# Early mLSTM convolutions, rotary tables on 128x128, and a planner that treats VectorE and GpSimd as exclusive

## The chip, the cores and the metric

The kernel runs on one core of a Trainium2 chip. The metric is the device time of one execution in microseconds (us); lower is better. A core has a matrix engine (TensorE, PE in the profile, with its weight loads as PEld), three engines for elementwise work (VectorE is DVE, ScalarE is ACT, GpSimd is POOL), and SyncE (SP), whose queue issues all the DMAs here. Each engine works through its own instructions in order and waits on semaphores of the others. Matmul results land in PSUM banks; all other tiles lie in SBUF.

## The reference

512 tokens of width 1024 pass through two blocks, all in float32. In the first, `u = rms_norm(h)` is multiplied by `w_in`, and the product is cut into the inputs of two mixers:

```python
# latent attention (MLA), 4 heads of 128 + 64 rotary columns
cos, sin = rope_cos_sin(positions)     # ang = positions[..., None] * inv_freq, 32 frequencies
q_pe, k_pe = apply_rope(q_pe, cos, sin), apply_rope(k_rope, cos, sin)
mla_out = causal_mla(q, k, v)
# mLSTM, 4 heads of 128
qk = silu(causal_dwconv(concat([m_q, m_k]), conv_w, conv_b))   # 4 taps, 1024 channels
hm = mlstm_chunkwise(mq, mk, m_v, m_i + gate_bias_i, m_f + gate_bias_f)
mlstm_out = sigmoid(m_o) * rms_norm(hm, mlstm_norm)
mix = concat([mla_out, mlstm_out]) @ w_out
```

A SwiGLU feed-forward part, a gated embedding and a second block of two layers (differential attention, a short convolution, and two squared-ReLU feed-forward parts) follow. They are most of the time and no line of theirs is changed.

## The kernel before

**Products.** A float32 matrix is split into a high and a low part (`hi` by a ScalarE copy, `lo = x - hi` by VectorE or GpSimd), and each product is three matmuls: `hi*hi`, `hi*lo` and `lo*hi` (`mm3`, L344 to L346). Weights arrive as `raw` tiles (six of them, 128x512, loaded over SP's queue), are split into `whl` tiles by the `converter`, and are multiplied by the split activations `a`. So each weight costs ScalarE a copy and VectorE or GpSimd a subtraction (L303) before PE can use its low part.

**The order of the work.** The program is written as many Python generators ("streams"). While it is built, a planner (`Sched`) keeps a clock for each engine, has a cost formula for each operation, and at each step emits the operation that can start first by its estimate; ties go by a stream's priority. That fixes each engine's order of instructions, and SP's queue of DMAs too. On the chip an engine can't leave that order: where an estimate was too short, everything behind it waits. A request `"vg"` (from `tt`, used for the low parts) can go to VectorE or to GpSimd; `start` compares their estimated ends with a handicap, `tune(("vg", s.shared), 0.2)`, which is -0.2 while `s.shared` is false and 0.2 once it is true. Requests of `stt`, `vtt` and `tt` carry a flag that both inputs lie in SBUF (`two`). Only from `block1_rest` on, when `s.shared` is set, is a GpSimd operation planned as excluding such a VectorE operation, by the clock `s.port`.

**The first 240 us**, which the change touches: `x_in` reads and splits x; `z_in`, `v_block` and `z_main` multiply by `w_in`. `rope_tables` (priority 2) builds the cosine table `C` and the sine table `Sn` from positions and frequencies: `positions` is broadcast to all 128 partitions, and a chain of dependent GpSimd operations on 128x512 (`pts`, a scaling; `ptt`, an addition) brings the angles into the range of the sine: 13 `pts` and 8 `ptt`. Then VectorE clamps and ScalarE makes `Sn` and `C`. The frequencies repeat every 32 partitions, so the 128 rows of `C` are four equal groups. `rope_key` and `rope_q` wait for the key `"rope"`; the rotated queries go through a DMA (`qr<-p`) before `scores` of the attention can use them. `main1` runs `z_main` for four conv inputs (tiles 0, 4, 1, 5, kept as `rawz` in `a` tiles) during the attention, and after `"roped"` for the other four (in `y` tiles) and four output gates; these projections are PE's reserve while the mixers wait for other engines.

When the attention is done its pool is closed, the mLSTM pool is opened, and `conv_silu` runs for the tiles 0, 4, 1, 5, 2, 6, 3, 7: one ScalarE instruction, three multiply-adds on VectorE (L316), a tanh on ScalarE, a last VectorE instruction, and the split into `qk`. `mlstm_core` of head h needs `qk` of the tiles h and 4 + h. Its decay matrix `bc` comes by DMA; `decay` adds the triangular mask `tri` on GpSimd (`ptt`, L312) and takes the exponent on ScalarE; `weigh` multiplies the scores in PSUM by it.

## Time and profile before

| | us |
|---|---|
| three runs: median (lowest to highest) | 1825.43 (1823.6 to 1826.53) |
| the profiled execution | 1826.98 |
| its span from first to last instruction | 1825.2 |
| PE busy in it | 1785.4 |
| VectorE busy | 1372.8 |
| ScalarE busy | 1007.5 |
| GpSimd busy | 208.8 |

The profiled execution took 1.8 us more than its span, and 1.55 us more than the median of the runs. An engine counts as busy from an instruction's start to its end; matmuls overlap, so a busy PE may still be slow. The granted clock (PEclk) is the mean share of TensorE's full 2.4 GHz that the throttle granted in a stretch; 0.50 is its lower level of 1.2 GHz. A row of waits names the engine that stood still, the tile and line it was to work on, and the instruction whose end released it.

### The profile page before, as it was taken

The page shows a single profiled execution, that of the slowest core. Times are in us where ns is not written, and L with a number is a line of the kernel's source. Part 1 is how long each engine was busy: PE and PEld are TensorE (multiplying, and loading weights), DVE is VectorE, ACT ScalarE, POOL GpSimd, SP SyncE. Part 2 cuts the span into 40 slices and gives each one's busy share as a digit, 9 for nine tenths or more (in the row PEclk, how much of TensorE's full clock was granted, in tenths as well). Part 3 has the DMA queues.
Part 4 walks back from the last instruction along what each step waited for, and adds up shares of the span by engine and source line. Part 5 has one row for each costly group of instructions (what it writes and reads, how often), then busy time and mean ns, then how long its engine had stood idle before and what let it go on. Part 6 is the DMA issues. An engine that isn't in the chain of part 4 may idle for free.

```text
span 1825.2 us, 33452 instructions
## 1 busy us (share of the span) xinstructions
PE 1785.4 (98%) x12610; PEld 1659.8 (91%) x12610; DVE 1372.8 (75%) x3042; ACT 1007.5 (55%) x2270; POOL 208.8 (11%) x217
## 2 busy tenths in 40 slices
PE   8998999999999999999999999999999999999997
PEld 6786798999999989999999999999999988889997
DVE  7779677878888868888686777776955378777784
ACT  7656766544445546666676444455522367444452
POOL 5216101000001012101001000001000000111100
PEclk9998999999999999999999999999999999999999
DMA  5223411333334322121222333333422032233331
GB/s 189 82 76 121 138 61 64 116 102 101 105 105 145 111 75 62 53 65 65 76 70 90 96 93 93 96 115 103 139 93 93 25 104 70 98 110 105 104 105 47
DMA packets 95946, 171.73 MB, mean 94 GB/s; under 512 B 11888, under 2 KB 15520, under 8 KB 95784
## 3 DMA queue, kind: packets, MB, share of 16 engines
q1 hardware_dynamic: 95784, 169.60, 29.1%
q8 instruction: 99, 1.62, 0.4%
q14 instruction: 63, 0.52, 0.1%
HBM read 166.12 MB, written 2.13 MB: 92 GB/s over the span
## 4 chain that ended last, share of the span: by engine, by line
PE 86%; DVE 7%; ACT 2%; POOL 2%; DMA 1%; issue 1%; SPq 0%; DVEq 0%; POOLq 0%; ACTq 0%
PE u L344 16%; PE u L345 16%; PE u L346 16%; PE t L346 12%; PE t L345 12%; PE t L344 11%; DVE whl L303 1%; PE t L1987 1%; DVE cv L316 1%; DVE ssum L303 1%; POOL y L312 1%; POOL y L321 1%; PE t L757 1%; DVE a L316 1%; DVE y L308 1%
## 5 line engine op out<-in xcount | busy, mean ns | idle before, releaser
L344 PE MATMUL u<-a,whl 128*128 128x256 f32 (+3 forms) x1860 | 593.4, 319 | 3.4 <-ACT a L289 2.4
L346 PE MATMUL u<-a,whl 128*128 128x256 f32 (+3 forms) x1860 | 587.7, 316 | 2.7 <-POOL y L1109 2.7
L345 PE MATMUL u<-a,whl 128*128 128x256 f32 (+3 forms) x1860 | 586.9, 316 | 1.1 <-DVE a L316 1.1
L289 ACT ACTIVATE whl<-raw 128x512 fp32r<-128x512 f32 (+1 forms) x658 | 388.4, 623 | 320.3 <-PE u L346 132.6
L303 DVE TENSOR_TENSOR whl<-raw,whl 128x512 fp32r<-128x512 f32 (+1 forms) x620 | 430.6, 714 | 125.8 <-ACT whl L289 123.8
L344 PEld LDWEIGHTS u<-a,whl 128*128 128x128 f32 x1860 | 351.4, 189 | 29.7 <-ACT a L289 2.6
L346 PEld LDWEIGHTS u<-a,whl 128*128 128x128 f32 x1860 | 350.4, 188 | 26.0 <-POOL y L1109 3.2
L345 PEld LDWEIGHTS u<-a,whl 128*128 128x128 f32 x1860 | 350.4, 188 | 25.7 <-DVE a L316 2.0
L344 PE MATMUL t<-a,whl 128*128 128x256 f32 (+3 forms) x888 | 261.1, 294 | 2.2 <-DVE t L308 1.5
L345 PE MATMUL t<-a,whl 128*128 128x256 f32 (+3 forms) x888 | 259.6, 292 | 1.3 <-DVE a L316 1.3
L346 PE MATMUL t<-a,whl 128*128 128x256 f32 (+3 forms) x888 | 259.8, 293 | 0.0
L345 PE MATMUL t<-T,whl 128*128 128x256 f32 (+1 forms) x656 | 185.6, 283 | 0.0
L344 PE MATMUL t<-T,whl 128*128 128x256 f32 (+1 forms) x656 | 184.7, 282 | 0.0
L346 PE MATMUL t<-T,whl 128*128 128x256 f32 (+1 forms) x656 | 184.6, 281 | 0.0
L344 PEld LDWEIGHTS t<-a,whl 128*128 128x128 f32 x888 | 168.1, 189 | 8.0 <-issue 1.9
L345 PEld LDWEIGHTS t<-a,whl 128*128 128x128 f32 x888 | 167.7, 189 | 6.7 <-DVE a L316 1.6
L346 PEld LDWEIGHTS t<-a,whl 128*128 128x128 f32 x888 | 167.7, 189 | 3.5
L308 DVE TENSOR_TENSOR y<-y,u 128x258 f32<-128x258 f32 (+2 forms) x192 | 96.7, 507 | 69.2 <-PE u L346 68.9
L344 PEld LDWEIGHTS t<-T,whl 128*128 128x128 f32 x656 | 124.0, 189 | 0.1
L346 PEld LDWEIGHTS t<-T,whl 128*128 128x128 f32 x656 | 124.0, 189 | 0.0
L345 PEld LDWEIGHTS t<-T,whl 128*128 128x128 f32 x656 | 123.7, 189 | 0.0
L303 DVE TENSOR_TENSOR ssum<-ssum,sqt 128x256 f32<-128x256 f32 (+3 forms) x145 | 65.9, 459 | 62.3 <-ACT sqt L289 60.1
(311 smaller groups left out, 2917.1 us busy)
## 6 DMA issues: line engine op xcount, KB each, us to landing
raw<-in_w_up SPq DMA_DIRECT2D x172, 256.0 KB, 3.1
raw<-in_w_dn SPq DMA_DIRECT2D x168, 256.0 KB, 3.0
raw<-in_w_in SPq DMA_DIRECT2D x128, 256.0 KB, 2.8
raw<-in_w_out SPq DMA_DIRECT2D x48, 256.0 KB, 2.7
raw<-in_w_gate SPq DMA_DIRECT2D x44, 256.0 KB, 2.7
h<-in_xT SPq DMA_DIRECT2D x16, 256.0 KB, 4.4
raw<-in_w_pleg SPq DMA_DIRECT2D x16, 256.0 KB, 3.0
bc<-rows_dram SPq DMA_DIRECT2D x4, 640.0 KB
```

Of the source, the lines that this page charges most:

```text
L289: s.nc.scalar.activation(out, in_, f, **k)
L303: (s.nc.gpsimd if e == "pool" else s.nc.vector).tensor_tensor(out, a, b, op)
L308: s.nc.vector.tensor_tensor(out, a, b, op)
L312: s.nc.gpsimd.tensor_tensor(out, a, b, op)
L316: s.nc.vector.scalar_tensor_tensor(out, a, c, b, op0, op1)
L321: s.nc.gpsimd.tensor_scalar(out, a, c, d, ALU.mult, ALU.add)
L344: mm(ps, wh, xh, start=start, stop=False, **k)
L345: mm(ps, wh, xl, start=False, stop=False, **k)
L346: mm(ps, wl, xh, start=False, stop=stop, **k)
L757: s.nc.tensor.transpose(ps[:, (i - j) * P:(i - j + 1) * P], al[i][:, c + j * P:c + (j + 1) * P], s.ident)
L1987: mm(banks[c][-1][0], q[r, e, qs], k[r, f, a:b], start=x == 0, stop=x == 2)
```

## The change

The planner applies the exclusion of GpSimd and VectorE from the start, and the handicap of a `"vg"` request is 0.2 throughout. The rotary tables are computed on 128x128: partition group b holds tokens 128b to 128b+127 for the 32 frequencies. Four DMAs bring the positions, twelve sine instructions of 32x128 (besides one Abs of 128x128) put the four token groups side by side into rows 0 to 31 of `C` and 0 to 63 of `Sn`, and four DMAs copy these rows into the others; three of these are waited for in turn. The convolution's arithmetic of the tiles 0, 4, 1, 5 becomes a stream `conv_early` of priority 5, spawned as soon as its input is there, with an `sqt` tile for the running sum; it writes its result over the raw input. `conv_silu` of these four only splits. The mask of `decay` becomes a `"vg"` request.

```diff
--- before.py
+++ after.py
@@ -60,7 +60,7 @@
     ('out1', 'hsq', 1): 2, ('out1', 'rs', 0): 4, ('out20', 'evac', 1): 0.3,
     ('out20', 'hide'): 3, ('out20', 'hsq', 0): 1, ('out20', 'lag'): 5,
     ('out20', 'op'): 0.2, ('out20', 'op1'): 1, ('out21', 'hsq', 0): 2,
-    ('out21', 'op'): 0.2, ('out21', 'op1'): 1, ('vg', False): -0.2,
+    ('out21', 'op'): 0.2, ('out21', 'op1'): 1,
     (('f2', 0), 'hsq', 1): 2, (('f2', 0), 'rs', 1): 4, (('f2', 1), 'evac', 1): 0.3,
     (('f2', 1), 'op'): 0.05, 'combine': 2.4, 'core': 0.5, 'late': 2, 'meta': 3,
     'mlasoft': 1.2, 'out': 2.1, 'ple': 3, 'silu': 1, 'values': 1.7, 'zmain': 1,
@@ -93,7 +93,7 @@
 
     def __init__(s):
         s.free = {"pe": 0.0, "act": 0.0, "dve": 0.0, "pool": 0.0, "dma": 0.0}
-        s.port, s.shared, s.phase = 0.0, False, 0
+        s.port, s.phase = 0.0, 0
         s.keys, s.slots, s.make = {}, {}, {}
         s.ready, s.on_key, s.on_slot = [], {}, {}
         s.seq, s.now, s.table = 0, 0.0, None
@@ -173,7 +173,7 @@
             d, p = max(st.at("dve"), s.free["dve"]), max(st.at("pool"), s.free["pool"], s.port)
             if r[3]:
                 d = max(d, s.port)
-            return (p, "pool", r[2]) if p + r[2] <= d + r[1] + tune(("vg", s.shared), 0.2) else (d, "dve", r[1])
+            return (p, "pool", r[2]) if p + r[2] <= d + r[1] + 0.2 else (d, "dve", r[1])
         cost = r[1] * (1.07 if r[0] == "pe" else 1.0)
         if r[0] == "act" and len(r) > 2 and r[2] in s.TABLES and r[2] not in s.SERVES[s.table]:
             cost += 1.28
@@ -196,7 +196,7 @@
         s.ready.remove(st)
         s.now = a
         s.free[eng] = a + cost
-        if s.shared and (eng == "pool" or eng == "dve" and st.req[-1] is True):
+        if (eng == "pool" or eng == "dve" and st.req[-1] is True):
             s.port = a + cost
         st.t = st.end = a + cost + LAT
         st.last = eng
@@ -684,14 +684,16 @@
 
     def rope_tables(s, pool):
         nc, A = s.nc, s.A
-        rc = pool.tile([P, 2], F32, name="ropec")
-        yield from s.dma(rc, A["ropec"], 1024)
-        yield "slot", "y", 5
-        C, Sn, ang, t, u = (s.make["y"]()[:, :S] for _ in range(5))
-        pi = (yield from s.get("p")).bitcast(I32)[:, :S]
-        yield from s.dma(pi, A["positions"].broadcast_to([P, S]), 2048 * P)
+        rc = pool.tile([P, 1], F32, name="ropec")
+        yield from s.dma(rc, A["ropec"], 512)
+        yield "slot", "y", 3
+        C, Sn, x = (s.make["y"]()[:, :S] for _ in range(3))
+        ang, t, u, pi = (x[:, P * i:P * i + P] for i in range(4))
+        pi = pi.bitcast(I32)
+        for b in range(4):
+            yield from s.dma(pi[32 * b:32 * b + 32], A["positions"][0:1, P * b:P * b + P].broadcast_to([32, P]), 512 * 32)
         yield from s.vec("tensor_copy", t, pi)
-        s.put("p")
         yield from s.pts(ang, t, rc[:, 0:1])
         magic = 12582912.0
         twopi = 2 * math.pi
@@ -708,12 +710,18 @@
             for c in parts:
                 yield from s.pts(u, t, -c * big)
                 yield from s.ptt(ang, ang, u, ALU.add)
-        yield "dve", 0.6
+        yield "dve", 0.2
         nc.vector.tensor_scalar(ang, ang, 3.1415925, -3.1415925, ALU.min, ALU.max)
-        yield from s.act(Sn, ang, AF.Sin, scale=rc[:, 1:2])
         yield from s.act(t, ang, AF.Abs)
-        yield from s.act(C, t, AF.Sin, scale=-1.0, bias=s.halfpi)
-        s.put("y", 3)
+        for b in range(4):
+            r, c = slice(32 * b, 32 * b + 32), slice(P * b, P * b + P)
+            yield from s.act(Sn[0:32, c], ang[r], AF.Sin, scale=-1.0)
+            yield from s.act(Sn[32:64, c], ang[r], AF.Sin)
+            yield from s.act(C[0:32, c], t[r], AF.Sin, scale=-1.0, bias=s.halfpi[r])
+        s.put("y")
+        s.spawn(s.dma(Sn[64:128], Sn[0:64], 2048 * 64))
+        for b in (1, 2, 3):
+            yield from s.dma(C[32 * b:32 * b + 32], C[0:32], 2048 * 32)
         s.dump("C", C)
         s.dump("Sn", Sn)
         s.C, s.Sn = C, Sn
@@ -880,21 +888,36 @@
         s.dump("bcol", s.bcol)
         s.set("gates")
 
-    def conv_silu(s, t):
-
-        yield "key", ("rawz", t)
+    def conv(s, t, a, out):
         raw = s.rawz[t]
-        hl = yield from s.get("qk")
-        a = yield from s.get("cv")
         yield from s.act(a, raw[:, 3:3 + S], AF.Identity, scale=s.vc("conv_w", 24 + t), bias=s.vc("conv_b", t))
         for j in range(3):
             yield from s.stt(a, raw[:, j:j + S], s.vc("conv_w", 8 * j + t), a, ALU.mult, ALU.add)
         r = raw[:, 0:S]
         yield from s.act(r, a, AF.Tanh, scale=0.5)
-        yield from s.stt(a, r, 1.0, a, ALU.add, ALU.mult)
-        s.rawz_done(t)
-        yield from s.split(hl, a, 0, S)
-        s.put("cv")
+        yield from s.stt(out, r, 1.0, a, ALU.add, ALU.mult)
+    def conv_early(s, t):
+        a = (yield from s.get("sqt"))[:, :S]
+        yield from s.conv(t, a, s.rawz[t][:, 0:S])
+        s.put("sqt")
+        s.set(("pre", t))
+    def conv_silu(s, t):
+        early = t in (0, 4, 1, 5)
+        yield "key", ("pre" if early else "rawz", t)
+        hl = yield from s.get("qk")
+        if early:
+            yield from s.split(hl, s.rawz[t][:, 0:S], 0, S)
+            s.rawz_done(t)
+        else:
+            a = yield from s.get("cv")
+            yield from s.conv(t, a, a)
+            s.rawz_done(t)
+            yield from s.split(hl, a, 0, S)
+            s.put("cv")
         s.qk[t] = hl
         s.set(("qk", t))
 
@@ -972,7 +995,7 @@
 
     def decay(s, h, j, bc, c0, tri):
         n = S - j * P
-        yield from s.ptt(bc[:, c0:c0 + P], bc[:, c0:c0 + P], tri, ALU.add)
+        yield from s.tt(bc[:, c0:c0 + P], bc[:, c0:c0 + P], tri, ALU.add)
         yield from s.act(bc[:, c0:c0 + n], bc[:, c0:c0 + n], AF.Exp, bias=s.bcol[:, j * 4 + h:j * 4 + h + 1])
         s.set(("decay", h, j))
 
@@ -1041,6 +1064,8 @@
             yield from s.vtt(r[:, 3:3 + S], ps, s.rs[:, XO:W], ALU.mult)
             s.put("u")
             s.rawz[t] = r
+            if t in (0, 4, 1, 5):
+                s.spawn(s.conv_early(t), tune("early", 5))
             s.set(("rawz", t))
         return done
 
@@ -1712,7 +1737,7 @@
         s.put("t2")
 
     def block1_rest(s, mix):
-        s.shared, s.phase = True, 1
+        s.phase = 1
         s.spawn(s.load_h(), 1)
         fin, pin, nf = [None] * KT, [None] * KT, [None] * KT
         up = lambda t, i: (("f1", "up", 0, t), i)
@@ -2319,8 +2344,7 @@
 
     a["ident"] = np.eye(P, dtype=np.float32)
     f = (10000.0 ** (-np.arange(0, 64, 2) / 64)).astype(np.float32)
-    sign = np.where(np.arange(P) % 64 < 32, -1.0, 1.0).astype(np.float32)
-    a["ropec"] = np.stack([np.tile(f, 4), sign], axis=1)
+    a["ropec"] = np.tile(f, 4)[:, None]
     i = np.arange(P)
     a["tri"] = np.where(i[None, :] < i[:, None], np.float32(NEG), np.float32(0))
     mk = np.zeros((P, S), np.float32)
```

## Rows read from the trace of the kernel before

**Rows 1.** The page, part 1: busy us (share of the span) and instructions.
```profile
PE 1785.4 (98%) x12610; PEld 1659.8 (91%) x12610; DVE 1372.8 (75%) x3042; ACT 1007.5 (55%) x2270; POOL 208.8 (11%) x217
```

**Rows 2.** Stretches: length, busy us (instructions) by engine, PEclk granted clock, DMA.
```profile
20.00:80.00 60.00, 55.46 (x242) 43.65 (x241) 52.15 (x92) 43.99 (x80) 31.84 (x30) 0.97 0.32 100
80.00:130.00 50.00, 49.47 (x277) 42.70 (x276) 31.46 (x92) 26.68 (x65) 7.58 (x16) 1.00 0.18 54
130.00:139.00 9.00, 9.00 (x41) 7.37 (x40) 8.79 (x13) 7.22 (x13) 3.92 (x6) 1.00 0.44 147
139.00:161.00 22.00, 13.39 (x48) 9.98 (x47) 20.35 (x25) 12.81 (x24) 15.94 (x15) 0.77 0.39 129
161.00:200.00 39.00, 38.09 (x182) 30.89 (x181) 35.08 (x52) 29.35 (x53) 14.07 (x14) 1.00 0.32 103
```

**Rows 3.** Waits of PE, 0 to 240 us: who, for whom, total, times, longest.
```profile
PE t L345 <- DVE qk L303: 3.1, 1, 3.1
PE u L346 <- POOL y L1109: 2.7, 1, 2.7
...
PE t L344 <- DVE bc L316: 2.4, 2, 2.1
...
PE t L1222 <- DMA qr<-p: 1.2, 1, 1.2
```

**Rows 4.** Lines of PE, 139 to 161 us: busy us, mean ns, idle before.
```profile
L344 PE MATMUL u<-a,whl 128*128 128x512 f32 x8 | 3.6, 447 | 0.0
```

**Rows 5.** Stretches within 154 to 165 us.
```profile
154.00:157.00 3.00, 0.92 (x3) 0.41 (x3) 3.00 (x5) 0.40 (x1) 0.82 (x1) 0.50 0.14 27
...
161.00:165.00 4.00, 4.00 (x25) 3.66 (x24) 3.79 (x6) 2.31 (x5) 2.31 (x2) 0.98 0.45 177
```

**Rows 6.** Timeline of POOL, 134 to 143 us: start, us, [idle before].
```profile
135.08 6.10 POOL L312 TENSOR_TENSOR bc<-bc,tri 128x128 f32<-128x128 f32 x8 [9.85 <-DMA bc<-rows_dram]
141.13 1.27 POOL L303 TENSOR_TENSOR whl<-raw,whl 128x512 fp32r<-128x512 f32 x1
```

**Rows 7.** Lines of DVE by form, 139 to 161 us.
```profile
L316 DVE SCALAR_TENSOR_TENSOR cv<-a,cv 128x512 f32<-128x512 f32 x4 | 5.9, 1528 | 1.1 <-ACT a L289 1.1
```

**Rows 8.** Instructions on tile cv, 100 to 240 us: min/median/max ns.
```profile
L316 DVE SCALAR_TENSOR_TENSOR cv<-a,V,cv x12: 744/752/952, 130.9 to 139.5; 128x512 f32<-128x512 f32 x12
...
L316 DVE SCALAR_TENSOR_TENSOR cv<-y,cv x8: 679/691/696, 170.5 to 217.7; 128x512 f32<-128x512 f32 x8
...
L289 ACT ACTIVATE cv<-a,V x4: 805/807/808, 130.1 to 132.2; 128x512 f32<-128x512 f32 x4
```

**Rows 9.** Timeline of DVE: the last of the four early conv inputs.
```profile
122.60 0.68 DVE L308 TENSOR_TENSOR a<-u,rs 128x512 f32<-128x512 f32 x1
```

**Rows 10.** Lines of POOL by form, 0 to 240 us.
```profile
L303 POOL TENSOR_TENSOR whl<-raw,whl 128x512 fp32r<-128x512 f32 x15 | 23.3, 1568 | 24.0 <-ACT whl L289 24.0
L312 POOL TENSOR_TENSOR bc<-bc,tri 128x128 f32<-128x128 f32 x16 | 12.5, 813 | 14.3 <-DMA bc<-rows_dram 9.9 <-DVE whl L303 4.5
L312 POOL TENSOR_TENSOR y<-y,y 128x512 f32<-128x512 f32 x8 | 12.2, 1520 | 0.7
L321 POOL TENSOR_SCALAR y<-y 128x512 f32<-128x512 f32 x12 | 10.2, 850 | 1.0
...
L321 POOL TENSOR_SCALAR p<-p,st 128x128 f32<-128x128 f32 x4 | 2.4, 604 | 28.1 <-DVE st L297 24.1 <-PE t L757 4.0
```

**Rows 11.** Timeline of DVE: the clamp of the angles.
```profile
50.04 0.70 DVE L712 TENSOR_SCALAR y<-y 128x512 f32<-128x512 f32 x1 [1.17 <-POOL y L312]
```

**Rows 12.** Timeline of ACT: the last step of the tables.
```profile
55.26 0.71 ACT L289 ACTIVATE y<-y,halfpi 128x512 f32<-128x512 f32 x1
```

**Rows 13.** Timeline of SP's queue, 16 to 61 us.
```profile
16.19 0.42 SPq L325 DMA_DIRECT2D p<-in_positions  x1
...
59.32 1.64 SPq L325 DMA_DIRECT2D raw<-in_w_in  x2
```

**Rows 14.** DMA issues: count, KB each, median us to landing.
```profile
qr<-p SPq DMA_DIRECT2D x8, 128.0 KB, 2.5
```

## The prediction

> **What bounds the kernel now.** I read the page's busy shares first: PE is busy in 98% of the span [rows 1]. So the kernel ends when PE has done a fixed amount of work, and a change off PE pays only what it takes from PE's pauses and slow stretches. The span less the busy time is 40 us (the table); that is all there is, besides time in which PE is busy but slow. Next I cut the start into stretches, because the change touches only the first 240 us. One is to be seen at once [rows 2]: from 139 to 161 us PE is busy 13.4 us of 22.0, at a mean granted clock of 0.77, while VectorE is busy 20.4 and GpSimd 15.9. The stretch before it has no pause, the one after it 0.9 us in 39.
>
> Then the waits of PE [rows 3]. Three end in this stretch: 3.1 us for the low part of `qk`, 2.7 us for something on GpSimd, and 2.1 us (of 2.4) for `bc`, which `weigh` must free. What the stretch would cost without them: it holds 48 matmuls. 24 are projections (one of their three lines shows 8) [rows 4], which in the stretch before follow each other every 9.00/41 = 0.22 us [rows 2], so 5.3 us. The other 24 are the scores of two heads with mixed widths; 25 matmuls of such a mix took 4.0 us at nearly full clock [rows 5], 0.16 each, so 3.8 us. That is 9.1 us of work in 22.0: **12.9 us are lost here**. The three waits are 7.9; the remaining 5.0 are small gaps and above all the clock, which after the pauses was granted at 0.50, its lower level, and was back at 0.98 only from 161 us on [rows 5].
>
> Why these waits: the 2.7 us end with GpSimd. Eight `decay` masks hold it from 135.08 to 141.13, and the low part of a weight stands behind them [rows 6]. The 3.1 us come from VectorE: the last instruction of the convolution takes 1.53 us there [rows 7], but 0.69 us as the median of the same form for the later tiles [rows 8]. In that time GpSimd runs subtractions with two SBUF inputs. The two engines hinder each other, which the planner does not know in this phase.
>
> **The change, part by part.** Durations come from the profiled execution, which took 1827.0 us in all, 1.8 more than its span and 1.6 more than the median of the runs. The sum is made against 1827.0 and the 1.6 taken off at the end.
>
> *Convolutions, out of the mLSTM's start.* One costs VectorE 3 x 0.75 + 0.69 = 2.9 us and ScalarE 0.81 us and a tanh of about the same [rows 8]. Four of them, 11.8 us of VectorE, leave the time after 130 us, and two splits stand where head 0 waited for two convolutions. The `qk` wait of 3.1 goes. With VectorE free sooner, I give half of the `bc` wait, 1.0.
>
> *Exclusive planning and `decay`.* The planner now sees that a subtraction on GpSimd blocks VectorE, so it hands it fewer weights, and masks can go to VectorE: the wait of 2.7 goes. The Trainium skill, "SBUF — State Buffer", section "Who interferes with whom", states that the shared port is an exclusive lock and that the loser blocks for the whole instruction. By that, a VectorE operation of 0.69 behind a GpSimd subtraction alone of 1.27 would take 1.96; the row has 1.53 [rows 7], so the trace agrees in kind but with a smaller price, and the new planner is somewhat too strict rather than too lax. By the rule's price the sum would gain some 0.4 us more per such operation; I use the row.
>
> *Clock.* The 5.0 us follow the waits. As 3.1 + 2.7 + 1.0 = 6.8 of 7.9 go, I let the same share of 5.0 go: 4.3. Together 11.1; less 0.5, because the mLSTM stretch behind it still loses 0.9 per 39 us [rows 2]. **Gain 10.6**, bounds 3.1 (only the `qk` wait goes) and 12.4.
>
> *Early convolutions, into the attention.* From 80 to 130 us VectorE is busy 31.5 of 50 us, ScalarE 26.7 [rows 2]; 18.5 us of VectorE's idle time stand against 11.8. Their priority is behind the attention's. But an instruction under way is not broken off, so each of 16 can hold a softmax step by up to 0.75 us, and the last of the four inputs is there only at 122.6 us [rows 9], a few us before the end of the attention. PE has projections in reserve as cover. **Loss 1.0**, bounds 0 and the whole 11.8, if that cover is gone.
>
> *Work from GpSimd to VectorE.* Of 15 weight subtractions and 16 masks on GpSimd before 240 us [rows 10] I let most go to VectorE: 15 x 0.69 = 10.4 us, and the masks at a quarter to a third of 0.69 for a quarter of the columns, 3 to 4 us. Against that stands what VectorE loses no more by blocking, 0.84 us for each such operation [rows 7, 8], and the 11.8 us that moved. **Loss 0.7**, bounds 0 and 5.
>
> *Rotary tables.* The chain on GpSimd is 12 x 0.85 + 1.6 + 8 x 1.52 = 24.0 us of work [rows 10] (the 1.6 stand for the first scaling, which has a column operand, taken at the price of an addition); it ends with the clamp at 50.0 [rows 11], and `C` is done at 56.0 [rows 12]. On 128 columns the nearest rows are 0.60 for a scaling and 0.81 for an addition [rows 10], both with VectorE beside them: 13 x 0.60 + 8 x 0.81 = 14.3; a quarter of the long ones would be 6. I take 12: 12 us sooner. Against it: twelve sine steps in place of two, at between 0.18 (a quarter of 0.71 [rows 12]) and 0.71 us, say 0.3, so about 2 us more; three copies of `C` waited for in turn, each about the 2.5 us of the `qr` copies [rows 14], 7 us; positions in four DMAs instead of the one at 16.19 [rows 13], which the planner spaces by 2 us, so 1 to 2 us later in the end. Net some 2 us sooner: **0** by itself, since rotated queries cost PE one wait of 1.2 us [rows 3]. Shorter blocking of VectorE from 24 to 50 us helps the latents; of the 4.5 us that PE pauses from 20 to 80 us [rows 2] I give back a third. **Gain 1.5**, bounds 0 and 4.5. Fewer `y` tiles held cost nothing, and no projection waited for one.
>
> The sum: 1827.0 - 10.6 - 1.5 + 1.0 + 0.7 = 1816.6; less 1.6 as the runs stand to the profile: **1815.0 us**. What lies behind 240 us keeps its policy; with the DMA engines busy for 0.18 to 0.44 in these stretches [rows 2] its weights can come sooner too, so a shift of 10 us should last to the end.
>
> **The rivals.**
> 1. *Half of the stall stays.* Scores need `bc`, whose DMA kept GpSimd waiting until 135 us [rows 6], then masks, exponents, `weigh`. If the planner again places scores too early, PE waits for `bc` (2.1) and runs slow after it (5.0): the gain is 3.1 + 2.7 = 5.8 in place of 10.6. For it: SP and VectorE are full there. Against: of eight projections with 24 matmuls each, more than five were still to come at 139 us (41 of the matmuls from 130 us on were all theirs) [rows 2]. Time 1815.0 + 4.8 = 1820, give or take 2.
> 2. *Slower: the tables come late.* The new DMAs stand in SP's queue between weight loads, which wait for a free `raw` tile; two of them are issued only at 59.3 [rows 13]. Copies of `C` that stand behind them land from 61 + 2.5 = 63.5 us on, and one of the three may stand behind a later pair and lose as much again: some 15 us later than 56.0 as an upper bound. The attention starts later by this, its four projections are used up before it, and what is late passes to the end: 1815 + 15 = 1830. It decides from 14 us on; below that it only eats the gain. For it: seven DMAs in series where there were two. Against: the shorter chain has 12 us in hand.
> 3. *Nothing gained.* The early convolutions are pushed back behind the attention by their priority, and other waits fill the stretch: PE's pauses move instead of going. Time 1824 to 1827. For it: the fourth input at 122.6 [rows 9]. Against: head 0 needs only the tiles 0 and 4, which come first.
>
> **How the numbers follow.** The forecast, 1807 to 1820, has 0.62; rival 1 0.20; rival 2 0.12; rival 3 0.06. A difference of 0.2%, 3.7 us, is about what a measurement of this kernel tells from none. Faster by that (below 1821.8): 0.62 + half of rival 1 = 0.72. Same: the other half and nearly all of rival 3, 0.15. Slower (above 1829.1): rival 2 and a little, 0.13. The range: below, 12.4 + 4.5 at their bounds with no losses give 1808.5, so I begin at 1807; above, it takes in rivals 1 and 3 and ends at 1827, leaving out rival 2 and a little below.
>
> **What would show it.** Right: between 130 and 165 us no wait of PE over 1 us and the clock at 1.00; L316 on tiles 0, 4, 1, 5 before 130 us; the sum of GpSimd's subtractions before 240 us well below 23 us; VectorE's two-input operations near 0.69 us; the sine rows before 56 us; the same 12,610 matmuls. Wrong: PE pauses of several us between 75 and 130 us with VectorE full (early convolutions too dear), the first use of rotated queries after 80 us (rival 2), or a slow clock that has only moved. A shift at 240 us that is lost again by 1800 us would mean that the end hangs on something else than PE.

## The result, and the profile after

| | before | after |
|---|---|---|
| median of four runs on the same chip (lowest to highest), us | 1825.57 (1823.6 to 1826.53) | 1807.28 (1805.38 to 1807.55) |
| profiled execution, us | 1826.98 | 1807.18 |
| its span, us | 1825.2 | 1805.4 |

The ratio is 0.9899, with a 95% interval of 0.9882 to 0.9916: 18.3 us faster. The prediction said 1815.0, in a range of 1807 to 1827; the result lies 0.3 us above the range's lower end. Part 1 of the page of after answers to [rows 1]:

```profile
PE 1780.7 (99%) x12610; PEld 1658.2 (92%) x12610; DVE 1358.4 (75%) x3066; ACT 1008.2 (56%) x2280; POOL 169.8 (9%) x193
```

The matmuls are the same 12,610. The span of the profiled execution is 19.8 us shorter and PE's busy time 4.7 us (1780.7 against 1785.4). So PE's idle time, span less busy, fell from 39.8 to 24.7 us: 15.1 us of the gain are pauses that are gone, and 4.7 us are the same work done in less busy time. The stretches of [rows 2] for the kernel after (length, busy us and instructions of PE, PEld, DVE, ACT, POOL, granted clock, DMA share, GB/s):

```profile
20.00:80.00 60.00, 59.96 (x274) 48.67 (x273) 49.26 (x100) 48.79 (x95) 15.38 (x31) 1.00 0.37 115
80.00:130.00 50.00, 50.00 (x280) 43.11 (x279) 39.80 (x108) 32.00 (x75) 9.57 (x15) 1.00 0.21 64
130.00:139.00 9.00, 6.79 (x31) 5.69 (x30) 8.81 (x19) 8.50 (x19) 4.60 (x5) 0.89 0.61 218
139.00:161.00 22.00, 22.00 (x96) 18.42 (x96) 17.87 (x37) 14.76 (x31) 3.43 (x4) 0.89 0.50 166
161.00:200.00 39.00, 39.00 (x187) 31.46 (x187) 28.73 (x48) 29.36 (x48) 5.91 (x5) 1.00 0.37 112
```

From 139 to 161 us PE now does 96 matmuls where it did 48, and stands still for no moment. But look at the first stretch too: 274 matmuls against 242, in the same 60 us. That is a gain as well, and a large one.

To place the gain, I count work and not busy time. For each matmul record, in order of start, its columns at 2.4 GHz plus 17 ns are added up, and two kernels are compared at the moments when their sums are equal. The difference is how far one is **ahead at equal work**. It comes from one profiled execution of each, so it is good to about 0.5 us. At 80 us of work (100.1 us on the clock of before) after is 8.5 us ahead; at 200 us of work (239.9 us on that clock) it is 18.3 ahead; at 300, 18.9; at 1200, 18.8; at 1700, 19.7. So the gain has two halves: **8.5 us in the front** and **9.8 us in the transition** from the attention to the mLSTM. Both last to the end. The last 0.8 us come near 1260 us of work, where PE waits 1.52 us for ScalarE before and 0.88 after; the instructions of each engine stand in the same order there in both kernels, so this is not the change's order.

The waits of PE from 0 to 240 us, all that the view names, which answer to [rows 3]:

```profile
PE t L344 <- DVE bc L316: 2.2, 1, 2.2
PE m L662 <- DVE ones L677: 1.2, 1, 1.2
PE u L344 <- ACT a L289: 0.9, 1, 0.9
PE u L345 <- DVE a L316: 0.3, 1, 0.3
```

The waits of 3.1 us for `qk` and 2.7 us for GpSimd are gone; the one for `bc` is as long as it was. Short stretches around it, same columns:

```profile
135.00:138.00 3.00, 0.80 (x5) 0.73 (x4) 3.00 (x9) 3.00 (x7) 0.64 (x1) 0.83 0.69 203
138.00:141.00 3.00, 3.00 (x12) 2.90 (x12) 2.46 (x7) 3.00 (x7) 1.92 (x3) 0.50 0.75 257
141.00:146.00 5.00, 5.00 (x18) 4.03 (x18) 3.97 (x8) 1.23 (x3) 1.40 (x1) 0.72 0.82 262
146.00:150.00 4.00, 4.00 (x25) 3.52 (x24) 2.97 (x9) 2.29 (x7) 0.00 (x0) 1.00 0.04 16
```

After three microseconds in which PE was busy for 0.80, the clock was granted at 0.50, the lower level of 1.2 GHz, and was back at 1.00 from 146 us on. Some of the old stall has moved from 139–161 to 135–146 us; it has not gone.

Where the parts went: the tile `sqt` of the early convolutions (min/median/max ns, first and last start):

```profile
L316 DVE SCALAR_TENSOR_TENSOR sqt<-a,V,sqt x12: 733/744/753, 71.2 to 115.0; 128x512 f32<-128x512 f32 x12
L289 ACT ACTIVATE sqt<-a,V x4: 807/815/817, 69.3 to 110.2; 128x512 f32<-128x512 f32 x4
L289 ACT ACTIVATE a<-sqt x4: 631/632/644, 74.9 to 117.3; 128x512 f32<-128x512 f32 x4
L316 DVE SCALAR_TENSOR_TENSOR a<-a,sqt x4: 680/686/693, 75.6 to 118.2; 128x512 f32<-128x512 f32 x4
```

All four run between 69 and 119 us; the last step takes 686 ns as the median, against the 1528 ns of [rows 7]. GpSimd by form, 0 to 240 us, against [rows 10]:

```profile
L303 POOL TENSOR_TENSOR whl<-raw,whl 128x512 fp32r<-128x512 f32 x10 | 13.7, 1380 | 45.3 <-ACT whl L289 45.3
L321 POOL TENSOR_SCALAR y<-y 128x128 f32<-128x128 f32 x12 | 5.4, 447 | 0.9
L312 POOL TENSOR_TENSOR y<-y 128x128 f32<-128x128 f32 x8 | 4.5, 564 | 0.6
```

Its weight subtractions fell from 15 to 10, its rotary chain from 24.0 to about 10 us, and the masks left it altogether. VectorE does them, in less time than GpSimd's 813 ns:

```profile
L303 DVE TENSOR_TENSOR bc<-bc,tri 128x128 f32<-128x128 f32 x16 | 3.5, 282 | 0.0
```

### The profile page after: what moved, and what is told of

It is laid out like the page before. It is cut to its first block, busy times and chain, and to the rows that moved or that the text cites. A ratio compares the mean times of both kernels' runs of the same rounds, so it can differ in the third digit from the quotient of the medians.

```text
span 1805.4 us, 33466 instructions
## 1 busy us (share of the span) xinstructions
PE 1780.7 (99%) x12610; PEld 1658.2 (92%) x12610; DVE 1358.4 (75%) x3066; ACT 1008.2 (56%) x2280; POOL 169.8 (9%) x193
## 4 chain that ended last, share of the span: by engine, by line
PE 92%; DVE 5%; ACT 1%; DMA 1%; issue 1%; SPq 0%; DVEq 0%; ACTq 0%
PE u L344 17%; PE u L345 17%; PE u L346 17%; PE t L345 12%; PE t L346 12%; PE t L344 12%; PE t L2012 1%; DVE whl L303 1%; DVE ssum L303 1%; PE t L765 1%; DVE a L316 1%; DVE y L316 1%; DVE h L303 0%; PE t L365 0%; ACT y L289 0%
## 5 line engine op out<-in xcount | busy, mean ns | idle before, releaser
L303 DVE TENSOR_TENSOR whl<-raw,whl 128x512 fp32r<-128x512 f32 x625 | 430.1, 708 | 129.6 <-ACT whl L289 127.4
```

Of the source, the lines that this page charges most:

```text
L303: (s.nc.gpsimd if e == "pool" else s.nc.vector).tensor_tensor(out, a, b, op)
```

## The experiments

Each median is of 4 to 11 executions, beside the kernel before on the same chip. "Ahead" is the lead over before at equal work, at 80 and at 200 us of it; a minus means behind.

| label | kernel | median us | before beside it | ratio (95%) | ahead at 80 | at 200 |
|---|---|---|---|---|---|---|
| `o_rope` | before, short tables only | 1825.15 | 1826.08 | 0.9993 (0.9985 to 1.0002) | -1.1 | 2.4 |
| `o_excl` | before, planning only | 1828.10 | 1826.08 | 1.0012 (1.0003 to 1.0021) | -2.0 | -3.9 |
| `o_conv` | before, early convolutions only | 1817.25 | 1826.08 | 0.9949 (0.9936 to 0.9963) | 0.5 | 10.7 |
| `o_off` | before, no early `vg` on GpSimd | 1825.04 | 1826.08 | 0.9998 (0.9989 to 1.0006) | 1.8 | 0.5 |
| `m_excl` | after, less planning | 1819.63 | 1826.50 | 0.9963 (0.9951 to 0.9976) | -1.5 | 7.3 |
| `m_rope` | after, less short tables | 1812.34 | 1826.50 | 0.9925 (0.9913 to 0.9938) | -1.9 | 11.7 |
| `m_conv` | after, less early convolutions | 1817.23 | 1826.50 | 0.9945 (0.9933 to 0.9958) | 8.6 | 10.5 |
| `o_bc` | before, 2.5 us more in an estimate | 1819.79 | 1826.50 | 0.9960 (0.9946 to 0.9973) | -0.4 | 7.0 |
| `o_rope_hold` | `o_rope`, sines behind the gates | 1820.71 | 1825.86 | 0.9971 (0.9960 to 0.9983) | 5.3 | 7.0 |
| `a_bc` | after, 2.5 us more in the estimate | 1808.31 | 1825.86 | 0.9903 (0.9890 to 0.9917) | 8.4 | 19.8 |
| `a_bc5` | after, 5.0 us more | 1805.40 | 1825.86 | 0.9891 (0.9877 to 0.9904) | 8.6 | 22.7 |
| `m_dec` | after, masks on GpSimd | 1809.31 | 1825.86 | 0.9908 (0.9892 to 0.9923) | 7.9 | 18.6 |

### One part alone, on the kernel before

**`o_rope`**: only the hunks of `rope_tables` and of `ropec`.

```diff
-        yield from s.act(Sn, ang, AF.Sin, scale=rc[:, 1:2])
...
+            yield from s.act(Sn[32:64, c], ang[r], AF.Sin)
...
+            yield from s.dma(C[32 * b:32 * b + 32], C[0:32], 2048 * 32)
```

> The kernel before with the rotary tables on 128x128 alone. The whole change gained 18.3 us: about 8.7 us before 80 us (equal PE work is done that much sooner) and about 9.5 us between 115 and 190 us. Theory 1 (lock): the early 8.7 us come from GpSimd's long chain holding VectorE from 24 to 50 us, so the shorter chain alone gives most of them: 1818, give or take 2. Theory 2 (order): they come from the planner, which now knows what VectorE can do; the short chain alone gives 0 to 2 us: 1824 to 1826. Under both the wait at 139 us stays.

Measured: 1825.15 us, no change: the time of theory 2, but not its course. The lead at equal work tells more: 4.8 us ahead at 40 us of work, 1.5 behind at 60. A gain is made and lost again. PE's waits from 50 to 80 us:

```profile
PE u L344 <- DVE h L316: 5.5, 1, 5.5
```

and ScalarE's timeline (start, us):

```profile
42.99 1.28 ACT L289 ACT_TABLE_LOAD   x1
...
54.10 1.28 ACT L289 ACT_TABLE_LOAD   x1
...
57.09 1.28 ACT L288 ACT_TABLE_LOAD   x1
58.38 0.72 ACT L289 ACTIVATE p<-p,onec 4x512 f32<-4x512 f32 x1
...
66.45 1.84 ACT L289 ACTIVATE h<-u,rcol 128x512 fp32r<-128x512 f32 x3
```

The short chain is ready so early that the sines (44.28 to 53.6) come before the exponent and the logarithm of the gates. ScalarE loads the table of the sine, then needs two more loads before the logarithm at 58.38; the copies of the values out of PSUM (`h<-u,rcol`) stand behind this until 66.45, and PE waits 5.5 us for the bank `u` that they free.

**`o_excl`**: the planner's exclusion and handicap only.

```diff
-        if s.shared and (eng == "pool" or eng == "dve" and st.req[-1] is True):
+        if (eng == "pool" or eng == "dve" and st.req[-1] is True):
```

> The kernel before with the exclusive planning and its handicap of 0.2 alone; decay stays on GpSimd. Theory 1 (lock): the long chain still holds VectorE, so little comes before 80 us, and between 115 and 190 us some 5 us, since fewer weight subtractions go to GpSimd: 1820. Theory 2 (order): 6 to 8 us before 80 us and 5 behind: 1812 to 1815.

Measured: 1828.10 us, slower by 0.1%, which neither theory had; its profiled execution was its longest, 1831.22. PE's longest wait in 0 to 240 us:

```profile
PE t L344 <- ACT qk L289: 13.8, 1, 13.8
```

What GpSimd and, below, ScalarE did in that time (timelines):

```profile
137.48 5.15 POOL L312 TENSOR_TENSOR bc<-bc,tri 128x128 f32<-128x128 f32 x8 [14.06 <-DMA bc<-rows_dram]
```

```profile
138.43 1.48 ACT L289 ACTIVATE bc<-bc,bcol 128x512 f32<-128x512 f32 x2 [2.21 <-POOL bc L312]
...
141.02 2.33 ACT L289 ACTIVATE bc<-bc,bcol 128x128 f32<-128x128 f32 x5 [0.35 <-POOL bc L312]
143.25 0.61 ACT L289 ACTIVATE whl<-raw 128x512 fp32r<-128x512 f32 x1
143.77 0.61 ACT L289 ACTIVATE a<-cv 128x512 f32<-128x512 f32 x1
```

Read the three together. The DMA of `bc`, issued at 130.77, lets GpSimd begin at 137.48; the masks hold the exponents on ScalarE until 143.3; and only then comes the tanh of the first convolution (`a<-cv`), for which VectorE, the split and PE wait. The same order stands in ScalarE's timeline of the kernel before:

```profile
140.79 0.81 ACT L289 ACTIVATE bc<-bc,bcol 128x256 f32<-128x256 f32 x2 [0.25 <-POOL bc L312]
141.51 2.18 ACT L289 ACTIVATE a<-cv 128x512 f32<-128x512 f32 x4
```

So there too the convolution's last steps began with a tanh that was stuck in ScalarE's queue, behind exponents whose masks began only when the DMA had landed; GpSimd had then been idle for 9.85 us [rows 6], the last 5.5 of them after the DMA was issued at 129.59.

**`o_conv`**: only `conv_early`, its spawn, and the cut of `conv_silu`.

```diff
+                s.spawn(s.conv_early(t), tune("early", 5))
```

> The kernel before with the four early convolutions alone. Both theories: nothing before 80 us; the wait of 3.1 us for the low part of qk and part of the slow clock behind it go, 5 to 6 us: 1820. Rival: with GpSimd's subtractions unplanned, the early convolutions only move VectorE's jam into the attention, and the time is 1824 or more.

Measured: 1817.25 us, 10.2 us in the transition (0.5 to 10.7) and nothing in the front. That is more than the 5 to 6 us expected: the early convolutions alone are worth the whole transition.

**`o_off`**: GpSimd gets none of the early `vg` work, with no other change.

```diff
-    ('out21', 'op'): 0.2, ('out21', 'op1'): 1, ('vg', False): -0.2,
+    ('out21', 'op'): 0.2, ('out21', 'op1'): 1, ('vg', False): -99,
```

> The kernel before, with the handicap of a shared request at -99 until the first feed-forward part, so that these requests never go to GpSimd there; no exclusion is planned, the rotary chain and decay stay on GpSimd. If it is enough to keep subtractions off GpSimd, the time is that of the exclusive planning alone, within 2 us. If what matters is that the planner knows when the rotary chain and decay hold VectorE, it is 3 us or more slower than the exclusive planning alone.

Measured: 1825.04 us, no change, and 3.1 us faster than `o_excl`, so neither case of the expectation came. Two weight subtractions are left on GpSimd before 240 us, and the hindrance is gone: VectorE's last four convolution steps take 2.50 us, where they took 5.9 [rows 7].

```profile
145.96 2.50 DVE L316 SCALAR_TENSOR_TENSOR cv<-a,cv 128x512 f32<-128x512 f32 x4 [0.70 <-ACT a L289]
```

And yet PE's wait for head 0's `qk` is longer, 5.8 us (a second one, of 5.3 us, follows at 167 us), and the tanh again stands on ScalarE behind the last exponent of `bc`:

```profile
145.01 0.40 ACT L289 ACTIVATE bc<-bc,bcol 128x128 f32<-128x128 f32 x1 [0.35 <-POOL y L1109]
145.31 2.17 ACT L289 ACTIVATE a<-cv 128x512 f32<-128x512 f32 x4
```

The prediction's cause is real, but it was not alone: when it goes, the other one binds. The two are not weighed against each other by this run, since the new order also issues `bc` later, at 133.62 where it was 129.59.

### One part taken out of the kernel after

```diff
 m_excl
+        if s.shared and (eng == "pool" or eng == "dve" and st.req[-1] is True):
 m_rope
+        yield from s.act(Sn, ang, AF.Sin, scale=rc[:, 1:2])
 m_conv
-                s.spawn(s.conv_early(t), tune("early", 5))
```

Each takes back the whole part of the change, as `o_excl`, `o_rope` and `o_conv` put it in; one line of each is shown.

> The changed kernel with the planner's part taken back (no exclusion before the first feed-forward part, handicap -0.2): early convolutions, short tables and the decay request stay. Alone, the tables gave 1 us, the planning lost 2 and the convolutions gave 9, 8 in sum against 18 together. Theory 1 (the planning is needed for the early 9 us): the work done by 80 us is as late as with the tables alone, so 1815 to 1818. Theory 2 (short tables and convolutions carry it all, the planning adds nothing): 1807 to 1810.

> The changed kernel with the rotary tables on 128x512 again. Theory 1 (the long chain is what holds VectorE back whatever the planner knows): PE's work by 80 us is as late as with the planning alone, some 2 us behind the kernel before, and the gain at 139 us stays: 1816 to 1819. Theory 2 (the planner plans around the chain once the convolutions are early): 1808 to 1811.

> The changed kernel with all convolutions after the attention again. With the planning alone PE waited 13.8 us for the qk of head 0: the tanh of the first convolutions stood on ScalarE behind the exponents of bc, which wait for masks, which wait for the DMA of bc. Theory 1 (this queue is what the early convolutions cure): the 9 us before 80 us stay and a wait of PE of 5 to 14 us comes back at 125 to 145 us: 1816 to 1822. Theory 2 (VectorE hindered by GpSimd made the wait, and the planning cures that): no such wait, 1808 to 1812.

Measured: 12.4, 5.1 and 10.0 us slower than after by the medians; the kernel before beside these three was 0.9 us slower than the one beside after. `m_excl` lies 1.6 us and `m_rope` 1.3 us outside the nearer range of their theories, `m_conv` in that of theory 1. Without the planning the front's lead is gone (-1.5), and the 5.5 us wait of `o_rope` is back:

```profile
PE u L344 <- DVE h L316: 5.5, 1, 5.5
```

Without the short tables the front's lead is gone too (-1.9). Without the early convolutions it is whole (8.6), and the transition brings 1.9 in place of 9.8. By 80 us of work the front therefore needs two parts together, each of which leaves nothing there alone; the transition needs the early convolutions, or (`o_bc` below, in part) another order. In `m_conv` the tanh stands behind the exponents as before, and PE waits 5.2 us (ScalarE's timeline):

```profile
134.07 1.92 ACT L289 ACTIVATE bc<-bc,bcol 128x512 f32<-128x512 f32 x4 [0.21 <-DVE bc L303]
135.90 0.61 ACT L289 ACTIVATE a<-cv 128x512 f32<-128x512 f32 x1
```

### An estimate, and an order on ScalarE

**`o_bc`** adds and removes no instruction, but lets the planner believe that `bc` lands 2.5 us later. By its formula the DMA takes about 3.95 us. Before, it was issued at 129.59 and the first reader, which waited for it, began 5.5 us later; in `o_excl` that took 6.7 us. In after it landed 3.8 us after its issue, as the planner had it. So the estimate was 1.5 us short for the kernel before, and the 2.5 us are more than that.

```diff
         yield from s.dma(bc, s.rows_dram[h:h + 1, 0:1280].broadcast_to([P, 1280]), 5120 * P)
+        yield "wait", 2.5
```

> The kernel before, with 2.5 us added to the planner's estimate for the landing of bc; no instruction is added or taken away. Theory 1 (ScalarE's order): masks and exponents of bc are planned after the tanh of the first convolutions, which no longer stand behind them; most of the 12.9 us between 139 and 161 us come back: 1815 to 1819. Theory 2 (VectorE hindered by GpSimd): the convolutions stay slow, the wait for qk stays within 1 us: 1823 to 1827.

Measured: 1819.79 us, 0.8 us above the range of theory 1; 7.4 us come from the transition (-0.4 to 7.0). GpSimd's timeline, and below it ScalarE's:

```profile
134.00 4.71 POOL L303 TENSOR_TENSOR whl<-raw,whl 128x512 fp32r<-128x512 f32 x3 [8.36 <-ACT whl L289]
138.67 6.55 POOL L312 TENSOR_TENSOR bc<-bc,tri 128x128 f32<-128x128 f32 x8
```

```profile
139.35 0.64 ACT L289 ACTIVATE a<-cv 128x512 f32<-128x512 f32 x1 [2.83 <-DVE cv L316]
141.51 0.63 ACT L289 ACTIVATE a<-cv 128x512 f32<-128x512 f32 x1 [1.52 <-DVE cv L316]
142.05 3.72 ACT L289 ACTIVATE bc<-bc,bcol 128x512 f32<-128x512 f32 x8
```

GpSimd is still idle for 8.36 us, but then splits three weights ahead of the masks, and on ScalarE two tanhs go ahead of the exponents. PE's waits of 2.7 us for GpSimd and 2.1 for `bc` are gone; those for `qk` (2.7, 1.0 and 0.3 us) are not shorter in sum than before. So the order that followed from the planner's estimate, on two engines, made more than half of the 12.9 us. A run with the 5.5 us that were measured was not made.

**`o_rope_hold`** is `o_rope` with the sines made to wait for the gates' last use of their table, aimed at ScalarE's order.

```diff
         yield from s.act(m, fr, AF.Relu, scale=-1.0)
+        s.set("gexp")
...
+        yield "key", "gexp"
         yield from s.act(t, ang, AF.Abs)
```

> The kernel before with the short tables alone, their ScalarE part held until the gates' first exponent and logarithm are emitted; the planner is as before. With the short tables alone the work was 4.8 us ahead at 50 us and 1 us behind at 80 us: ScalarE did the sine steps first, loaded two tables more for the gates, and evacuated the values late, so PE waited 5.5 us for a bank. Theory 1 (what the planning adds at the start is this order on ScalarE): 6 to 8 us ahead at 80 us, and 1818 to 1820 in all. Theory 2 (it is that subtractions are kept off GpSimd): no more than 2 us ahead, 1823 to 1826.

Measured: 1820.71 us, 5.3 us ahead at 80 where `o_rope` was 1.1 behind; lead and time miss theory 1 by 0.7 us each and are far from theory 2. So 6.4 of the 9.6 us between `o_rope` and after come with that order: one table load (51.80), and the values copied from 63.41 on.

**`a_bc` and `a_bc5`** put the same line into after, with 2.5 and 5.0 us.

```diff
+        yield "wait", 5.0
```

> The changed kernel with 2.5 us added to the planner's estimate for the landing of bc. Theory: what is left of the stall, a wait of 2.2 us for bc at 135 us and the slow clock behind it, comes from head 1's scores being placed before bc can be there; with the truer estimate projections come first: 1802 to 1805. Rival: the order behind it gives the gain back, 1806 to 1809.

> The changed kernel with 5.0 us added to that estimate. Theory: more than is true, so no wait for bc either, but the two heads start later and projections run out before the last heads: 1803 to 1808, no better than with 2.5.

Measured: 1808.31 and 1805.40 us. The first, in the range of its rival, is no better than after, so that what a longer estimate gave before it does not give again, although it is 1.5 us ahead of it at 200 us of work; against before it loses 0.8 from 240 to 300 and 1.2 at 1200 to 1300 us. From 222 us on the instructions of every engine stand in the same order in `a_bc` as in after, so a shifted order is not the cause of these losses; what is stays open. The second has the lowest median of all (in its range, though expected to be no better than the first), 4.4 us ahead of after at 200 us of work, but its interval overlaps with that of after: it is not shown to be faster.

**`m_dec`** puts the masks back on GpSimd.

```diff
-        yield from s.tt(bc[:, c0:c0 + P], bc[:, c0:c0 + P], tri, ALU.add)
+        yield from s.ptt(bc[:, c0:c0 + P], bc[:, c0:c0 + P], tri, ALU.add)
```

> The changed kernel with the masks of decay on GpSimd again. Theory 1 (GpSimd has little else there now, but each mask of 128x128 takes twice as long beside VectorE): 1 to 3 us slower, 1808 to 1811. Theory 2 (masks on GpSimd hold up ScalarE's exponents as before): 4 us or more slower, with a longer wait of PE for bc.

Measured: 1809.31 us, 2.0 more than after and in the range of theory 1, but 18.6 us ahead at 200 us of work, as after is. What it loses it loses later, 1.6 us of it between 240 and 300 us, where there are no masks any more and each engine has the same order as in after. So this part of the loss arises neither at the masks nor from a shifted order there, and its cause stays open. The wait of 2.7 us for GpSimd does not come back (the longest are 2.4 for ScalarE and 2.3 for `bc`).

## Why the prediction was right, and where it was mis-sized

**The sum.** Against 1827.0 the prediction took off 10.6 in the transition and 1.5 in the front and added 1.0 and 0.7. Measured by equal work, the transition gave 9.8 with both losses in it (predicted: 8.9 net) and the front 8.5. With 9.8 + 8.5 in their place the sum is 1808.7 for the profiled execution, which took 1807.18; the other 1.5 us came after 200 us of work. The 1.6 us that the prediction took off at the end belonged to one execution of before: after's profiled execution (1807.18) lies at its median (1807.28).

**The range held by luck.** Its lower end was built from the upper bounds of both gains, with no losses: 1808.5, and then taken down to 1807 without a reason. The result, 1807.28, lies below 1808.5. So the path and the direction were right, and the transition was sized within 1 us, though not by the parts that were to earn it (below); but the whole gain of 18.3 us was 1.8 times the 10.4 that were forecast, because of the front.

**The front was the mis-sized term: 1.5 predicted, 8.5 measured, beyond the upper bound of 4.5.** I took the 4.5 us of PE's pauses from the busy share of [rows 2] as all that could be won from 20 to 80 us. For 139 to 161 us I had counted matmuls; here I did not. The same row says 242 matmuls, and after does 274 there. At 60/274 = 0.219 us each, the 32 are 7.0 us. Another 1.1 us had been won before 20 us (at 10 us of work). PE was busy for 55.46 of those 60 us, but part of that time it was slow. This stretch shows it, before and after:

```profile
50.00:60.00 10.00, 8.73 (x31) 6.88 (x31) 9.73 (x19) 9.15 (x16) 0.46 (x2) 0.83 0.17 54
50.00:60.00 10.00, 10.00 (x45) 8.11 (x44) 8.13 (x20) 7.06 (x16) 0.00 (x0) 1.00 0.37 110
```

31 matmuls in 10 us at a granted clock of 0.83, and 45 at 1.00. The Trainium skill, "Perfetto Trace Analysis", section "Identifying the Most-Contended Engine", says that the busy share of the matmuls is not a good measure of how close a kernel is to its limit, because pipelined instructions of PE look smaller in the trace, and names the busy share of the weight loads as one of two better ones. The trace agrees: from 20 to 80 us the weight loads were busy for 43.65 us before [rows 2] and 48.67 after, a rise of 11.5% where the number of matmuls rose by 13% and PE's busy time by 8%. In the freely running stretch from 130 to 139 us they were busy for 7.37 of 9.00 us [rows 2]; by that share 43.65 us are worth 53.3, and 6.7 of the 60 us were lost: near the 7.0, and not the 4.5.

**Where the front's lead comes from.** The prediction's mechanism, a VectorE less hindered by the rotary chain while the latents are made, is seen in the rows; it was its size that was off. VectorE by form, 30 to 50 us, before and then in `o_rope`:

```profile
L308 DVE TENSOR_TENSOR h<-h,h 128x512 f32<-128x512 f32 x2 | 2.7, 1368 | 0.0
L316 DVE SCALAR_TENSOR_TENSOR a<-h,V,a 128x512 fp32r<-128x512 f32 x2 | 2.5, 1267 | 1.8 <-ACT a L289 1.8
```

```profile
L308 DVE TENSOR_TENSOR h<-h,h 128x512 f32<-128x512 f32 x2 | 1.4, 684 | 0.0
L316 DVE SCALAR_TENSOR_TENSOR a<-h,V,a 128x512 fp32r<-128x512 f32 x3 | 2.3, 752 | 2.3 <-ACT a L289 2.2
```

By 50 us of work the kernels with the short chain are 3.8 to 6.8 us ahead (`o_rope` 4.8, after 6.8 of its 8.5), those with the long one -3.0 to 2.3, and this is before the copies of the values have begun. How much of it is the shorter VectorE operations and how much another order is not separated. What `o_rope` lacks is the second half: keeping that lead.

**The rotary tables, counted as 0.** At 80 us of work they are by themselves worth that: `o_rope`. The chain was shortened more than I said, from 24.0 to 10.3 us (0.37 + 5.4 + 4.5) where I took 12 off. But the positions come in four DMAs, which SP issued from 15.07 to 25.75, so the chain begins later: its clamp runs at 45.11, 4.9 us earlier than [rows 11]. ScalarE's timeline after:

```profile
42.72 0.71 ACT L289 ACTIVATE p<-p,onec 4x512 f32<-4x512 f32 x1
...
45.82 1.28 ACT L289 ACT_TABLE_LOAD   x1
47.12 0.63 ACT L289 ACTIVATE y<-y 32x128 f32<-32x128 f32 x2
...
53.54 0.40 ACT L289 ACTIVATE y<-y,halfpi 32x128 f32<-32x128 f32 x1
...
60.37 0.69 ACT L289 ACTIVATE h<-u,rcol 128x512 fp32r<-128x512 f32 x1
```

I gave 0.3 us to a sine step; it has 0.31, or 0.40 with the bias. The copies of `C` and `Sn` are issued from 53.96 to 57.5, and `C` is first used at 59.78, where it was 59.26 before: 0.5 us later, not 2 sooner. That cost nothing visible. What I did not see was ScalarE, which has the gates' logarithm, the sines and the copies of the values in one queue. From the timelines of ScalarE (us at the start; "ahead" at 50 and at 80 us of work):

| kernel | gates' logarithm | last sine | first copy of the values | ahead at 50 | at 80 |
|---|---|---|---|---|---|
| after | 42.72 | 53.54 | 60.37 | 6.8 | 8.5 |
| `m_conv` | 42.77 | 53.59 | 60.41 | 6.8 | 8.6 |
| `o_rope_hold` | 49.35 | 58.80 | 63.41 | 3.8 | 5.3 |
| `o_off` | 50.79 | 56.01 | 65.51 | 2.3 | 1.8 |
| `o_rope` | 58.38 | 53.21 | 66.45 | 4.8 | -1.1 |
| before | 49.53 | 55.26 | 66.98 | 0 | 0 |
| `m_excl` | 59.28 | 54.10 | 67.35 | 3.9 | -1.5 |
| `m_rope` | 41.64 | 59.80 | 69.25 | 0.7 | -1.9 |
| `o_excl` | 42.95 | 61.50 | 70.98 | -3.0 | -2.0 |

The copies follow PE's own progress, so their order in the table is in part the lead itself. What they cost shows between 50 and 60 us of work. The 50th was reached at 59.8 us in after and at 61.8 in `o_rope`; the first copy comes 0.6 us later in after and 4.7 us later in `o_rope`. It is over 3 us late in `o_rope`, `m_excl` (4.7) and `m_rope` (3.3) alone, and these three lose 6.3, 5.7 and 2.2 us by 60 us of work, while after, `m_conv` and `o_rope_hold` win another 1.6 to 2.0. And the table shows why neither part works alone: with the short tables the logarithm is late (58.38), with the planning the sine is (61.50), since the planner then spaces the long chain out (its clamp runs at 59.26, not at 50.04); with both, each is early.

**The early convolutions, 1.0 lost.** None is to be seen: PE is busy for 50.00 of 50 us from 80 to 130, with VectorE at 39.80 in place of 31.46. The cover held.

**GpSimd's work to VectorE, 0.7 lost.** Also nothing to be seen. 16 masks went over at 0.28 us each, and VectorE is nevertheless less busy from 139 to 161 us, 17.87 us against 20.35.

**Why these waits.** The 2.7 us were as predicted, a weight behind eight masks; what the prediction did not say is why the masks stood there: they were ordered ahead of the weights by an estimate that had their DMA land 1.5 us sooner than it did, after 9.85 idle us of GpSimd [rows 6]. `o_bc` removes that wait by a longer estimate alone. I credited it to the planning and the masks' move; `o_conv` is rid of it without either, and `m_dec` without the move. For the 3.1 us I was half right. The hindrance of VectorE by GpSimd costs what [rows 7] shows, but without it (`o_off`) the wait is 5.8, with the tanh behind the exponents. The early convolutions win because they take the tanh, and the arithmetic behind it, out of that queue before `bc` is in it.

**Exclusive planning.** I gave it the whole wait of 2.7. Alone it costs 2 us; with the short tables it keeps the lead that these make and adds 2.0 us by 50 us of work (4.8 in `o_rope`, 6.8 in after), and so turns -1.1 at 80 us into 8.5. The three parts alone add up to 0.9 - 2.0 + 8.8 = 7.7 us (the masks were not tried alone), and with the masks they give 18.3.

**The rivals.** Rival 1 came true in its kind: the wait for `bc` stays (2.2 us), and the clock behind it costs 3.0 x 0.50 + 5.0 x 0.28 = 2.9 us more, so the forecast of no wait over 1 us and a clock of 1.00 was wrong, and the prediction's own sign of being wrong, a slow clock that has only moved, came in part. That leaves 12.9 - 5.1 = 7.8 of the 10.6; most of what is missing was made up because the losses of 1.0 and 0.7 did not come and the neighbouring stretches ran without pauses (50.00 and 39.00 us where [rows 2] has 49.47 and 38.09), 9.2 of the measured 9.8. Rival 2 did not come: the copies were issued between the weight loads at 49.69 and 58.05. Nor did rival 3: the early convolutions were over at 118.9.

**Left open.** That the lead is lost by ScalarE's order is shown by one run that was made for it (`o_rope_hold`), which moves the sines, and with them the gates and the copies; a run that moves the copies alone was not made. Of the 3.2 us between `o_rope_hold` and after, 3.0 are there already at 50 us of work, before the copies, so they are not the copies' doing; what the planning does for them is not separated.

## What to carry to other kernels

Count the work that PE does in a stretch (matmuls, or columns, against a stretch that runs freely) before bounding what can be won there; here the pauses were 4.5 us, and the missing matmuls 7.0. Where a planner or a hand sets the order of in-order queues, an estimate that is too short for a DMA can put a whole dependent chain ahead of work that was ready, on several engines at once (1.5 us too short went with some 7 us lost here), so follow a stall through every queue, and not only the one whose semaphore came last. Try parts alone and also each one's removal, and look at the lead along the way: here two were worth nothing alone and 8.5 us together, but one of them had made 4.8 us and lost them again.

## What the runs showed of the hardware

- A broadcast of 640 KB from DRAM rows to 128 partitions landed 3.5 to 3.8 us after its issue in after, and 7.7 in `o_excl`, as the second of two issued 0.4 us apart; the `qr` copies of 128 KB took 2.5 [rows 14].
- VectorE operations with two SBUF inputs were slower while GpSimd ran the rotary chain on 128x512: 1368 ns against 684 for a product, and 1267 against 752 for a multiply-add (before and `o_rope`, 30 to 50 us).
- Small tiles save less than their size on ScalarE: a sine with a bias column took 0.40 us on 32x128 and 0.71 on 128x512 [rows 12], which has four times the columns. GpSimd's additions and scalings on 128 columns averaged 0.56 and 0.45 us, against 1.52 and 0.85 on 512 [rows 10].
- A table load on ScalarE took 1.28 us, and the instruction behind it started at once (42.99 + 1.28 = 44.27, next at 44.28).
